# Differential attention: score matmuls over all 128 rows in place of half-height pairs

## The chip, the cores and the metric

The kernel runs on one core of a Trainium2 chip. The metric is the device time of one execution in microseconds (us), as the median over several runs. A core has TensorE (PE: matmuls, with a separate row PEld for the loads of the stationary operand), VectorE (DVE), ScalarE (ACT), GpSimd (POOL) and SyncE (SP), each with a queue of its own that it works off in order, and 16 DMA engines that these queues can start.

## The reference

A trunk of two layers, each with a half-step SwiGLU feed-forward net, a token mixer and a second half-step net, with adaptive modulation and layer norms around them; 512 positions, width 1024, float32. The mixer of the first layer is a bidirectional state-space scan; that of the second is differential attention, which is where the change lies. Cut to this part:

```
qkv = u @ w_qkv                              # u: 512 x 1024
q, k: (512, 8 heads, 2 maps, 64);  v: (512, 8 heads, 128)
s = einsum('bqhmd,bkhmd->bhmqk', q, k) / 8   # per head two maps, contraction over 64
s = s - slope[h] * |pos_q - pos_k|
p = softmax(s)
w = p[map 0] - lam * p[map 1]
o = rms_norm(w @ v, subln_g) * (1 - lambda_init);  out = o @ w_out
```

## The kernel before

All activations lie transposed, features on the 128 partitions and 512 positions along the columns. To keep float32 accuracy with float32r operands, every operand is split in two parts: hi, a rounded copy that ACT writes, and lo = x - hi, which DVE writes. A product is then three matmuls, hi x hi, hi x lo and lo x hi (`mm3`, line 160 of the profile, for all projections). `split_act` and `split_into` make the two parts from a PSUM tile (lines 147 and 148 without a scale, 151 and 152 with one).

Tiles are allocated from pools by a tag. `big` gives 128 x 512 tiles from a pool of 32; PSUM has 8 banks: four "acc" for projections, two "mid", two "ln". The order of the instructions on each engine is not the order of the source: a planner of the framework sets it when the program is built, from priorities in source order, a model of the durations and the free slots of the pools. On the chip each queue is then fixed and works with semaphores.

Attention (`attention`) loops over 8 heads. For each head, `unit_qk(h, 0)` projects q (24 matmuls of 128 x 512, for the two maps at once: map 0 on partitions 0 to 63, map 1 on 64 to 127) and scales it by 1/8, `unit_qk(h, 1)` projects k. The units of head h + 1 are interleaved with the four steps of head h. One step (`score_step`) takes 128 queries: it makes the scores of both maps against all 512 keys, in one "mid" bank for each map. There are six matmuls: for each pair of parts (hi, hi), (hi, lo) and (lo, hi) one for each map, with 64 rows of the stationary and of the moving operand each, rows 0 to 63 for map 0 and rows 64 to 127 for map 1 (line 933). DVE adds the distance term and takes the row maximum (line 936, one for each map), ACT the exponential (943), DVE normalizes and subtracts the maps (944 to 947). `turn_step` transposes the result on PE (955) and splits it (147, 148); `values` multiplies with V on PE (160), takes squares on ACT and sums them on PE (972), POOL takes the power of -1/2 (241), PE broadcasts it (247), DVE scales (978, tile "o"), and a split follows. Weights come through SP's queue (line 93) and are split by lines 117 and 118; POOL starts no DMA in this kernel.

Of the kernel before, what the change touches and what calls it, by code (L numbers as in the profile page):

```python
# [9 lines left out]
F32 = mybir.dt.float32  # L10
F32R = mybir.dt.float32r
AF = mybir.ActivationFunctionType
ALU = mybir.AluOpType
# [33 lines left out]
def hybrid_trunk(tc, xT, cb, par, cst, adaw, wgu, wdn0, wdn1, wdn2, wdt, win, wso, wqk, wv, wao, dist_in, dtp, lam_in, out):  # L47
    nc = tc.nc
# [13 lines left out]
    def big(dt=F32, name="big"):  # L62
        return ap.tile([P, T], dt, tag="a", name=name)

    def tmp(name="tmp"):
        return tp.tile([P, T], F32, tag="t", name=name)

    def acc(tag="acc"):
        return ps.tile([P, T], F32, tag=tag, name=tag, bufs=BANKS[tag])
# [21 lines left out]
    def load(src, n=1024):  # L91
        raw = wp.tile([P, 1024], F32, tag="raw", name="raw", bufs=4)
        nc.sync.dma_start(raw[:, :n], src)
        return raw[:, :n]
# [6 lines left out]
    def split(raw, where=None):  # L101

        n = raw.shape[-1]
        if where == "a":
            hi, lo = [], []
            for o in range(0, n, T):
                r = raw[:, o : o + T]
                h, l = big(F32R, "wah"), big(F32R, "wal")
                x = nc.scalar.activation(h, r, AF.Copy)
                y = nc.vector.tensor_tensor(out=l, in0=r, in1=h.bitcast(F32), op=ALU.subtract)  # L110
                for a, b in zip((x, y), behind):
                    tc.add_manual_dep(a.ins, b.ins.name, NOSYNC, reason="inputs before weights")
                hi.append(h)
                lo.append(l)
            return [(hi[c // T][:, c % T : c % T + P], lo[c // T][:, c % T : c % T + P]) for c in range(0, n, P)]
        hi, lo = ring()
        nc.scalar.activation(hi[:, :n], raw, AF.Copy)  # L117
        nc.vector.tensor_tensor(out=lo[:, :n], in0=raw, in1=hi[:, :n].bitcast(F32), op=ALU.subtract)  # L118
        return Unit(hi, lo, n)
# [20 lines left out]
    def split_act(src, scale=None):  # L140
        hi, lo = big(F32R, "hi"), big(F32R, "lo")
        split_into(hi, lo, src, scale)
        return hi, lo

    def split_into(hi, lo, src, scale=None):
        if scale is None:
            x = nc.scalar.activation(hi, src, AF.Copy)
            y = nc.vector.tensor_tensor(out=lo, in0=src, in1=hi.bitcast(F32), op=ALU.subtract)  # L148
            return x, y
        else:  # L150
            nc.scalar.activation(hi, src, AF.Copy, scale=scale)
            nc.vector.scalar_tensor_tensor(
                out=lo, in0=src, scalar=scale, in1=hi.bitcast(F32), op0=ALU.mult, op1=ALU.subtract
            )
# [11 lines left out]
    def proj(o, w, u, m=P, cols=FULL, prev=None):  # L166
        for a, b in cols:
            prev = mm3(
                o[:m, a:b], [(w[k][0], w[k][1], u[k][0][:, a:b], u[k][1][:, a:b]) for k in range(len(u))], prev
            )  # L170
        return prev
# [706 lines left out]
    def attention(n):  # L878
# [8 lines left out]
        for j in range(2):  # L887
            nc.vector.scalar_tensor_tensor(
                out=lt[:, 256:320], in0=lt[:, 128 * j : 128 * j + 64], scalar=1.0, in1=lt[:, 128 * j + 64 : 128 * j + 128],
# [8 lines left out]
        qks, V = {}, {}  # L898

        def unit_qk(h, e, cols=FULL, pre=None):  # L900
            def f():
                pp = acc()
                proj(pp, pre or split(load(wqk[h, e])), u, cols=cols)
                qks[h, e] = split_act(pp, 0.125 if e == 0 else None)
            return f

        def unit_v(p_):
# [14 lines left out]
            return f  # L922

        def score_step(h, i, bt):
            (qh, ql), (kh, kl) = qks[h, 0], qks[h, 1]
            sm = sp.tile([P, 8], F32, tag="sm", name="sm", bufs=4)
            ss, pt = [acc("mid") for _ in range(2)], []
            c = slice(i * P, (i + 1) * P)

            for j, (a, b) in enumerate(((qh, kh), (qh, kl), (ql, kh))):  # L930
                for m in range(2):
                    r = slice(m * 64, m * 64 + 64)
                    nc.tensor.matmul(ss[m], lhsT=a[r, c], rhs=b[r, :], start=j == 0, stop=j == 2)  # L933
            for m in range(2):
                p = tmp("p")
                nc.vector.tensor_tensor_reduce(
                    out=p, in0=ss[m], in1=bt[:, 384 - i * P : 896 - i * P], scale=1.0, scalar=-3.0e38,
                    op0=ALU.add, op1=ALU.max, accum_out=sm[:, m : m + 1],
                )
                pt.append(p)  # L940
            nc.vector.tensor_scalar(out=sm[:, 2:4], in0=sm[:, 0:2], scalar1=-1.0, scalar2=None, op0=ALU.mult)
            for m in range(2):
                nc.scalar.activation(pt[m], pt[m], AF.Exp, bias=sm[:, 2 + m : 3 + m], accum_out=sm[:, 4 + m : 5 + m])
            nc.vector.reciprocal(sm[:, 6:8], sm[:, 4:6])
            nc.vector.tensor_tensor(out=sm[:, 7:8], in0=sm[:, 7:8], in1=nlam, op=ALU.mult)
            nc.vector.tensor_scalar(out=pt[0], in0=pt[0], scalar1=sm[:, 6:7], scalar2=None, op0=ALU.mult)
            nc.vector.scalar_tensor_tensor(
                out=pt[0], in0=pt[1], scalar=sm[:, 7:8], in1=pt[0], op0=ALU.mult, op1=ALU.add
            )
            return pt[0]  # L950
# [46 lines left out]
        for h in range(8):  # L997
            bt = bp.tile([P, 896], F32, tag="bt", name="bt")
            nc.scalar.activation(bt, dist, AF.Copy, scale=-(2.0 ** -(h + 1)))
            wh = bp.tile([P, 4, T], F32R, tag="wth", name="wth")  # L1000
            wl = bp.tile([P, 4, T], F32R, tag="wtl", name="wtl")
            todo = []
            if h < 7:
                todo += [unit_qk(h + 1, e) for e in range(2)]
            if h in (1, 3, 5):
                todo.append(unit_v((h + 1) // 2))
            if h == 7:
                todo.append(outp)
            for i in range(4):
                w = score_step(h, i, bt)  # L1010
                back.append(lambda i=i, w=w, wh=wh, wl=wl: turn_step(i, w, wh, wl))
                if i == 3:
                    back.append(lambda h=h, wh=wh, wl=wl: values(h, wh, wl))
                    back.append(lambda: rests.pop(0)())
                if todo:
                    todo.pop(0)()
                while len(back) > 2 and not (h == 7 and i == 3):
                    back.pop(0)()
# [10 lines left out]
    for d in range(KT):  # L1029
# [9 lines left out]
        for o in (hl[0], uf):  # L1039
            x = nc.scalar.activation(o, res[d], AF.Identity, bias=shift[0][:, d : d + 1], scale=onep[0][:, d : d + 1])  # L1040
# [122 lines left out]
```

## Time and profile before

| | |
|---|---|
| median of 3 runs | 2211.13 us (2209.78 to 2213.06) |
| the profiled execution, its own time | 2214.77 us |
| its span, first to last instruction | 2213.0 us |
| granted TensorE clock, mean | 0.993 |
| PE, PEld busy | 2156.0 us (97%), 1858.7 us (84%) |
| DVE, ACT, POOL busy | 1701.8 us (77%), 1059.4 us (48%), 136.2 us (6%) |
| DMA queues | 88384 packets, 294.81 MB on the one hardware queue; no software queue |

Busy times are shares of the whole span. Attention takes from about 1570 to 1830 us of it. Matmuls are pipelined: the recorded duration of one overlaps with the next, so what a matmul takes of PE's time is read from start to start.

### The profile page before, as it was taken

To read this page: it belongs to the slowest core of one execution; us is meant where nothing else is said; L and a number is where in the kernel's file an instruction comes from. 1 tells how busy PE (TensorE), PEld (TensorE's weight loads), DVE (VectorE), ACT (ScalarE), POOL (GpSimd) and SP (SyncE) were. 2 spreads that over 40 slices of the span, in tenths; PEclk is the share of its full clock that TensorE was granted. 3 is DMA by queue.
4 is the path that set the end of the run, shared out by engine and by line. 5 is a ranking of instruction groups with operands and counts; after the bars stand their busy time and mean duration, and the time that the engine had idled before them with its cause. 6 is when DMAs were issued, how large, how long until landed. Compare 5 with 4: busy or idle time off the path is not lost.

```text
span 2213.0 us, 33554 instructions
## 1 busy us (share of the span) xinstructions
PE 2156.0 (97%) x13030; PEld 1858.7 (84%) x13030; DVE 1701.8 (77%) x2948; ACT 1059.4 (48%) x1766; POOL 136.2 (6%) x226
## 2 busy tenths in 40 slices
PE   7999999999999989999999999999999999999998
PEld 5788888966777779989899989899877779989897
DVE  6865568656666689989889988997766689859697
ACT  4422234767656537434355524343845557425253
POOL 0000000034332300000000000000000000000000
PEclk9999999999999999999999999999999999999999
DMA  8865552375445413545543273733211121323231
GB/s 309 284 210 172 189 193 80 100 188 146 143 134 152 120 57 124 195 148 184 169 129 114 84 256 100 245 101 117 69 58 58 58 67 59 124 67 116 86 123 40
DMA packets 88543, 296.95 MB, mean 134 GB/s; under 512 B 9536, under 2 KB 12992, under 8 KB 88384
## 3 DMA queue, kind: packets, MB, share of 16 engines
q1 hardware_dynamic: 88384, 294.81, 41.6%
q8 instruction: 102, 1.67, 0.3%
q14 instruction: 57, 0.47, 0.1%
HBM read 289.53 MB, written 5.24 MB: 133 GB/s over the span
## 4 chain that ended last, share of the span: by engine, by line
PE 78%; DVE 10%; ACT 4%; DMA 3%; issue 3%; POOL 1%; POOLq 0%; ACTq 0%; SPq 0%; DVEq 0%
PE acc L160 64%; PE mid L160 6%; PE mid L783 2%; DMA raw<-in_adaw 1%; DVE raw L178 1%; PE mid L933 1%; DMA raw<-in_wdn 1%; DVE wl L118 1%; DVE raw L459 1%; PE ln L160 1%; DVE wl L450 1%; PE ln L247 1%; POOL E L772 1%; DVE lo L148 1%; PE ln L731 1%
## 5 line engine op out<-in xcount | busy, mean ns | idle before, releaser
L160 PE MATMUL acc<-hi,wh 128*128 128x512 f32 (+1 forms) x1488 | 504.0, 339 | 7.8 <-DVE resid L366 5.3
L160 PE MATMUL acc<-hi,wl 128*128 128x512 f32 (+1 forms) x1488 | 502.7, 338 | 0.0
L160 PE MATMUL acc<-lo,wh 128*128 128x512 f32 (+1 forms) x1488 | 502.1, 338 | 0.0
L160 PE MATMUL acc<-uh,wh 128*128 128x512 f32 (+1 forms) x1256 | 441.4, 352 | 0.1
L160 PE MATMUL acc<-ul,wh 128*128 128x512 f32 (+1 forms) x1256 | 438.9, 350 | 0.8 <-DVE ul L1041 0.8
L160 PE MATMUL acc<-uh,wl 128*128 128x512 f32 (+1 forms) x1256 | 437.5, 349 | 0.8 <-DVE wl L118 0.8
L117 ACT ACTIVATE wh<-raw 128x1024 fp32r<-128x1024 f32 (+1 forms) x234 | 238.8, 1026 | 399.8 <-PE acc L160 212.0
L118 DVE TENSOR_TENSOR wl<-raw,wh 128x1024 fp32r<-128x1024 f32 (+1 forms) x234 | 277.9, 1188 | 83.4 <-ACT wh L117 74.1
L160 PEld LDWEIGHTS acc<-hi,wh 128*128 128x128 f32 x1488 | 281.4, 189 | 44.2 <-issue 5.5
L160 PEld LDWEIGHTS acc<-lo,wh 128*128 128x128 f32 x1488 | 281.4, 189 | 31.1 <-DVE lo L148 1.2
L160 PEld LDWEIGHTS acc<-hi,wl 128*128 128x128 f32 x1488 | 281.5, 189 | 30.7 <-issue 1.2
L449 ACT ACTIVATE wh<-raw 128x1024 fp32r<-128x1024 f32 x162 | 170.7, 1059 | 213.8 <-DVE raw L459 100.0
L160 PEld LDWEIGHTS acc<-uh,wh 128*128 128x128 f32 x1256 | 237.1, 189 | 40.0 <-issue 8.9
L160 PEld LDWEIGHTS acc<-uh,wl 128*128 128x128 f32 x1256 | 237.3, 189 | 34.6 <-issue 3.9
L160 PEld LDWEIGHTS acc<-ul,wh 128*128 128x128 f32 x1256 | 237.4, 189 | 34.3 <-issue 4.4
L450 DVE TENSOR_TENSOR wl<-raw,wh 128x1024 fp32r<-128x1024 f32 x162 | 196.9, 1219 | 29.8 <-ACT wh L449 28.7
L178 DVE SCALAR_TENSOR_TENSOR raw<-raw,cond 128x1024 f32<-128x1024 f32 x144 | 174.7, 1221 | 55.7 <-DMA raw<-in_adaw 54.9
L366 DVE SCALAR_TENSOR_TENSOR resid<-acc,gv,resid 128x512 f32<-128x512 f32 (+1 forms) x172 | 112.4, 659 | 72.7 <-PE acc L160 72.5
L459 DVE TENSOR_TENSOR raw<-raw 128x512 f32<-128x512 f32 x216 | 148.0, 688 | 4.5
L312 POOL TENSOR_TENSOR rr<-vr,mhalf 128x2 f32<-128x2 f32 x12 | 8.8, 732 | 1545.2 <-DVE vr L308 1545.2
L160 PE MATMUL mid<-uh,wh 128*128 128x256 f32 (+2 forms) x332 | 94.9, 286 | 1.9 <-DVE up L491 1.9
L160 PE MATMUL mid<-uh,wl 128*128 128x256 f32 (+2 forms) x332 | 93.9, 283 | 0.0
(264 smaller groups left out, 3724.5 us busy)
## 6 DMA issues: line engine op xcount, KB each, us to landing
raw<-in_wgu SPq DMA_DIRECT2D x176, 512.0 KB, 4.2
raw<-in_adaw SPq DMA_DIRECT2D x144, 512.0 KB, 4.5
raw<-in_wdn SPq DMA_DIRECT2D x64, 448.0 KB, 3.6
raw<-in_win SPq DMA_DIRECT2D x40, 512.0 KB, 3.6
raw<-in_wdn SPq DMA_DIRECT2D x32, 512.0 KB, 4.5
rw<-scr SPq DMA_DIRECT2D x32, 512.0 KB, 5.4
ch<-scr SPq DMA_DIRECT2D x32, 256.0 KB, 3.5
raw<-in_wso SPq DMA_DIRECT2D x16, 512.0 KB, 3.5
```

Of the source, the lines that this page charges most:

```text
L117: nc.scalar.activation(hi[:, :n], raw, AF.Copy)
L118: nc.vector.tensor_tensor(out=lo[:, :n], in0=raw, in1=hi[:, :n].bitcast(F32), op=ALU.subtract)
L148: y = nc.vector.tensor_tensor(out=lo, in0=src, in1=hi.bitcast(F32), op=ALU.subtract)
L160: last = nc.tensor.matmul(o, lhsT=a, rhs=b, start=start and j == 0, stop=j == n - 1, skip_group_check=not start)
L178: nc.vector.scalar_tensor_tensor(out=raw, in0=raw, scalar=1.0, in1=cond, op0=ALU.mult, op1=ALU.mult, accum_out=mods[l][:, j : j + 1],)
L247: nc.tensor.matmul(o[:, j * P : (j + 1) * P], lhsT=cols[:, j : j + 1].broadcast_to([P, P]), rhs=ident, start=True, stop=True)
L366: nc.vector.scalar_tensor_tensor(out=res[d][:, a:b], in0=pd[:, a:b], scalar=gvec[n][:, d : d + 1], in1=res[d][:, a:b], op0=ALU.mult, op1=A ...
L449: nc.scalar.activation(x[0], r, AF.Copy)
L450: nc.vector.tensor_tensor(out=x[1], in0=r, in1=x[0].bitcast(F32), op=ALU.subtract)
L459: nc.vector.tensor_tensor(out=o, in0=x, in1=y, op=ALU.add)
L731: nc.tensor.matmul(pst, lhsT=bt[:, i * P : (i + 1) * P], rhs=xd, start=o == 0, stop=o == 1)
L783: nc.tensor.matmul(py[hh * 64 : (hh + 1) * 64, cc], lhsT=lhs, rhs=rhs, start=k == 0, stop=k == 2)
```

## The change

For each map of a head, k becomes one tile of 128 partitions: the hi part on the map's own 64 partitions and the lo part on the other 64. q becomes two tiles for each map: hi, and lo, each present on both halves of the partitions; ACT and DVE write the map's own half, and a DMA that POOL starts copies it to the other half. A contraction over 128 rows with the hi tile of q then gives hi x hi + hi x lo, and one with the lo tile lo x hi + lo x lo. So a step has four matmuls of full height, two for each map, the first map's ahead of the second's; the term lo x lo, which the kernel before leaves out, comes with it. The space for the descriptors of software DMAs goes from 1024 to 2048.

```diff
@@ unit_qk, def f @@
                 pp = acc()
                 proj(pp, pre or split(load(wqk[h, e])), u, cols=cols)
-                qks[h, e] = split_act(pp, 0.125 if e == 0 else None)
+                qks[h, e] = []
+                for m in range(2):
+                    r, o = (slice(j * 64, j * 64 + 64) for j in (m, 1 - m))
+                    if e == 1:
+                        k = big(F32R, "kk")
+                        nc.scalar.activation(k[r], pp[r], AF.Copy)
+                        nc.vector.tensor_tensor(out=k[o], in0=pp[r], in1=k[r].bitcast(F32), op=ALU.subtract)
+                        qks[h, e].append(k)
+                    else:
+                        hi, lo = big(F32R, "qh"), big(F32R, "ql")
+                        split_into(hi[r], lo[r], pp[r], 0.125)
+                        for x in (hi, lo):
+                            nc.gpsimd.dma_start(x[o].bitcast(F32), x[r].bitcast(F32))
+                        qks[h, e].append((hi, lo))
             return f
@@ score_step @@
-            (qh, ql), (kh, kl) = qks[h, 0], qks[h, 1]
             sm = sp.tile([P, 8], F32, tag="sm", name="sm", bufs=4)
             ss, pt = [acc("mid") for _ in range(2)], []
             c = slice(i * P, (i + 1) * P)
-
-            for j, (a, b) in enumerate(((qh, kh), (qh, kl), (ql, kh))):
-                for m in range(2):
-                    r = slice(m * 64, m * 64 + 64)
-                    nc.tensor.matmul(ss[m], lhsT=a[r, c], rhs=b[r, :], start=j == 0, stop=j == 2)
+            for m in range(2):
+                for j, q in enumerate(qks[h, 0][m]):
+                    nc.tensor.matmul(ss[m], lhsT=q[:, c], rhs=qks[h, 1][m], start=j == 0, stop=j == 1)
@@ kernel @@
-    nc = bacc.Bacc("TRN2", target_bir_lowering=False, num_devices=1, dynamic_dma_scratch_size=1024)
+    nc = bacc.Bacc("TRN2", target_bir_lowering=False, num_devices=1, dynamic_dma_scratch_size=2048)
```

## Rows read from the trace of the kernel before

**Rows 1.** Page, part 1: busy us, share of the span, instructions.

```profile
PE 2156.0 (97%) x13030; PEld 1858.7 (84%) x13030; DVE 1701.8 (77%) x2948; ACT 1059.4 (48%) x1766; POOL 136.2 (6%) x226
```

**Rows 2.** Windows, two heads: length, PE, PEld, DVE, ACT, POOL busy, clock, DMA.

```profile
1673.00:1731.00 58.00, 57.61 (x329) 45.30 (x328) 40.08 (x98) 30.74 (x61) 2.01 (x2) 1.00 0.17 55
```

**Rows 3.** Timeline of PE, a projection's second matmul: start, duration, instruction.

```profile
1579.51 0.39 PE L160 MATMUL acc<-ul,wh 128*128 128x512 f32 x1
```

**Rows 4.** Timeline of PE, from the projection's last matmul over one score step.

```profile
1584.53 0.39 PE L160 MATMUL acc<-uh,wl 128*128 128x512 f32 x1
1584.84 0.50 PE L933 MATMUL mid<-hi 64*128 64x512 f32 x2
1585.18 0.40 PE L933 MATMUL mid<-lo,hi 64*128 64x512 f32 x2
1585.41 0.40 PE L933 MATMUL mid<-hi,lo 64*128 64x512 f32 x2
1585.74 0.50 PE L160 MATMUL acc<-uh,wh 128*128 128x512 f32 x1
1586.08 0.40 PE L160 MATMUL acc<-ul,wh 128*128 128x512 f32 x1
```

**Rows 5.** Timeline of PE, a step whose second map starts later.

```profile
1653.40 0.50 PE L933 MATMUL mid<-hi 64*128 64x512 f32 x1
...
1653.80 0.49 PE L933 MATMUL mid<-hi 64*128 64x512 f32 x1
...
1654.69 0.50 PE L160 MATMUL acc<-uh,wl 128*128 128x512 f32 x1
```

**Rows 6.** Timeline of PE, a step in three pieces.

```profile
1637.77 0.50 PE L933 MATMUL mid<-hi 64*128 64x512 f32 x1
1638.20 0.49 PE L160 MATMUL ln<-wth,hi 128*128 128x512 f32 x1
1638.62 0.49 PE L933 MATMUL mid<-hi 64*128 64x512 f32 x1
...
1639.05 0.50 PE L160 MATMUL ln<-wtl,hi 128*128 128x512 f32 x1
...
1641.82 0.73 PE L933 MATMUL mid<-hi,lo 64*128 64x512 f32 x2
1642.48 0.50 PE L160 MATMUL acc<-uh,wh 128*128 128x512 f32 x1
```

**Rows 7.** Groups by line and shape, 1560 to 1833: count, busy us, mean ns.

```profile
L148 DVE TENSOR_TENSOR lo<-acc,hi 128x512 fp32r<-128x512 f32 x16 | 11.0, 685 | 0.1
L147 ACT ACTIVATE hi<-acc 128x512 fp32r<-128x512 f32 x16 | 9.4, 588 | 3.8 <-PE acc L160 3.8
```

**Rows 8.** Timeline of all engines, about a k split: in brackets the idle time before.

```profile
1651.19 0.68 DVE L148 TENSOR_TENSOR lo<-acc,hi 128x512 fp32r<-128x512 f32 x1
...
1651.79 0.74 DVE L978 SCALAR_TENSOR_TENSOR o<-o,l,ln 128x512 f32<-128x512 f32 x1
...
1652.44 0.68 DVE L936 CUSTOM_DVE_ANT_0 p<-mid,bt 128x512 f32<-128x512 f32 x1
...
1652.58 0.42 PEld L955 LDWEIGHTS ln<-csts,p 128*128 128x128 f32 x4 [0.56 <-DVE o L978]
...
1653.05 0.68 DVE L936 CUSTOM_DVE_ANT_0 p<-mid,bt 128x512 f32<-128x512 f32 x1
```

**Rows 9.** Timeline of POOL and PE, one head's power and its broadcast.

```profile
1644.11 1.01 POOL L241 TENSOR_TENSOR rr<-rv,mhalf 128x4 f32<-128x4 f32 x1 [32.64 <-DVE rv L239]
...
1648.98 1.05 PE L247 MATMUL ln<-csts,rr 128*128 128x128 f32 x8
```

**Rows 10.** DMA issues by line: count, KB each, median us from issue to landing.

```profile
lam<-in_lam SPq DMA_DIRECT2D x1, 128.0 KB, 3.8
```

**Rows 11.** Timeline of DVE and PE, head 0: q's subtraction and the first step.

```profile
1570.86 0.69 DVE L152 SCALAR_TENSOR_TENSOR lo<-acc,hi 128x512 fp32r<-128x512 f32 x1 [1.47 <-ACT hi L151]
...
1578.28 0.50 PE L933 MATMUL mid<-hi 64*128 64x512 f32 x2
```

## The prediction

> **What bounds the kernel now.** The page's first part comes first: TensorE (PE) is busy for 97% of the span, VectorE (DVE) for 77% [rows 1]. A busy PE says little by itself, since matmuls overlap, so the stage that is changed was read next, by windows. [...] The third view is PE's timeline, read from start to start, since a recorded duration contains the overlap with the next matmul.
>
> **The price of a full-height matmul.** From the second of a projection's 24 matmuls (start 1579.51, [rows 3]) to the last (1584.53, first of [rows 4]) are 22 intervals in 5.02 us: 0.228 us each for 128 rows and 512 columns.
>
> **What the six half-height matmuls cost.** The two maps use rows 0 to 63 and 64 to 127, and the rows come in pairs ("x2"): a pair starts within one slot, 0.34, 0.23 and 0.33 us after one another [rows 4]. The six therefore do not take six slots, and "four in place of six" is not a saving of a third. They take three slots, of which the first and last are stretched, and the neighbours pay too: the full-height matmul ahead has 0.31 us to the next start instead of 0.228 (+0.08), and the one behind 0.34 (+0.11). With 0.90 us for the step itself, an unbroken step costs 0.08 + 0.90 + 0.11 = 1.09 us. [...]
>
> Of the 32 steps (8 heads, 4 blocks of queries), 17 have this form. In 8, the second map starts 0.40 us behind the first, as its PSUM bank is still being read, and the pairs come apart [rows 5]: 1653.40 to 1654.69 is 1.29, with the neighbours 1.29 + 0.08 + 0.11 = 1.48. In 3, the planner has laid full-height matmuls between pieces of a step [rows 6]: 0.43 + 0.43 + 0.66 for the pieces, 0.42 - 0.228 = 0.19 for the lone full-height one in between, two more entries at 0.08 and two exits at 0.11, together 2.09. The last 4 are in two pieces; I price them as the 8. Sum: 17 x 1.09 + 12 x 1.48 + 3 x 2.09 = 18.5 + 17.8 + 6.3 = 42.6 us.
>
> **What takes their place.** 32 steps of four matmuls of the shape that the projections around them have: 128 x 0.228 = 29.2 us, wherever the planner puts them, since there is no other height to change to. PE's queue gets shorter by 42.6 - 29.2 = 13.4 us. This is a choice: the trace shows no full-height matmul in this place, and I take the projection's. The bounds are 0.228 and the 0.34 that each first one after a change takes; the second would make it 43.5, no gain at all.
>
> Not all of it arrives. In the 8 steps of [rows 5] the wait for the bank stays: DVE's two reads of the scores start 0.61 us apart (1652.44 and 1653.05, [rows 8]), the first map's two matmuls cover 0.46 of that, so 0.15 us x 8 = 1.2 us remain (0 if DVE is earlier, as the first map's scores are now ready two slots sooner).
>
> **The splits of q and k.** Each of the 16 units had one ACT copy (0.588 us) and one DVE subtraction (0.685, [rows 7]); both are now made twice on 64 partitions with the same 512 columns. I take the full duration for half the partitions, since every row of the trace has its time from the columns; below that, half. DVE gets 16 operations more, at its spacing of 0.60 us (1651.19 to 1651.79, [rows 8]) 9.6 us; ACT 16 x 0.588 = 9.4 us. Over a 58 us stretch DVE goes from 40.1 to 42.5 (four units), ACT from 30.7 to 33.1, so neither becomes the bound on average. What counts is where PE waits behind one: in [rows 8] the k subtraction runs at 1651.19, the head's output scaling (o, L978) behind it at 1651.79, and PE's transposes sat idle 0.56 us until it freed their bank. A second subtraction in front makes this 0.60 longer. This stands once in each of three such stretches, and one like it in head 1: 4 x 0.60 = 2.4 us. Ends: 0 (the planner places them elsewhere) and all 16 pairs exposed, 9.6 + 9.4 = 19.0. I take 2.4, as PE has its own work queued at the other places.
>
> **The transfers.** Per head POOL issues four DMAs, 64 partitions x 2 KB each, that copy q's parts to the other half. The trace has no DMA from POOL. Nearest rows: POOL's only work here takes 1.01 us [rows 9], and a transfer of the same 128 KB lands 3.8 us after its issue [rows 10]. Four in a row are then 4 x 1.01 + 3.8 = 7.8 us. For heads 1 to 7, q is projected beside the first step of the head before; the key projection (24 x 0.228 = 5.5 us) and three more steps lie between, so nothing waits. In POOL's queue stands also the power for the output norm; four issues ahead of it cost at most 4 us, and its broadcast comes at 1648.98 on PE, 3.9 us after the power ended at 1645.12 [rows 9]: covered but for a tenth. Head 0 has no such lead: its subtraction starts at 1570.86 and the first step at 1578.28 [rows 11]. With the second subtraction, 1570.86 + 0.69 + 0.60 + 7.8 = 1580.0 for the last part, which is read by the last of the four matmuls, at 1578.28 + 3 x 0.228 = 1579.0: 1.0 us late, behind which wait the next head's projection and all of PE. Ends: 0 and 5 us (issues twice as dear). [...] The larger descriptor scratch is space only.
>
> **Sum.** -13.4 + 1.2 + 2.4 + 1.0 = -8.8 us. The profiled execution took 2214.8 us (span 2213.0), so its successor would take 2206.0; that execution is 3.6 above the median of the runs, 2211.1, and against the median the time is 2202.3 us. Clock and everything ahead of attention stay.
>
> **Rivals.**
> *Given back (about the same).* The gain is there on PE, but the planner's new order and the longer splits eat it: with 8 to 12 of the 19.0 us exposed instead of 2.4, the sum is -3 to +1, 2208 to 2212 us. For it: DVE's queue is strictly in order and PE already waits on it in [rows 8]. Against it: DVE has 18 us of room in 58.
> *Four slots for three (slower).* Pairs in different row groups run at once, so three slots become four: 32 x 0.228 = 7.3 us more, if the stretched intervals are not due to the height and stay with the score step (their banks, their operands). With the 2.4 and 1.0 that is +10.7, 2221.8 us. It decides from a step of four at 1.19 us with its neighbours: (42.6 - 4.6) / 32, with the losses of the sum. For it: the pairs are plain in [rows 4]. Against it: all long intervals there stand at a change of height, the middle one is 0.23. [...]
> *The splits become the bound (slower).* All 16 pairs exposed (19.0) and head 0 at 5: -13.4 + 1.2 + 19.0 + 5 = +11.8, 2222.9. Against it: [rows 2].
> *More than forecast.* Nothing waits: -13.4, 2197.7.
>
> **How the numbers follow.** Two kernels can be told apart here from about 0.2%, 4.4 us. The forecast (a gain of 5 to 13 us) has 0.68, nothing waits at all 0.04; given back 0.16; four slots 0.06; the splits as the bound 0.06. So faster 0.72, same 0.16, slower 0.12. The range reaches from the whole gain with a little more, 2196, to the end of "given back", 2213, and leaves out the slower cases and a little below.
>
> **What would show it.** In the changed profile the score line should have 128 matmuls of 128 rows, 0.23 us from start to start and 0.23 to their neighbours, no "x2" pairs; two-head stretches of about 55.5 us instead of 58; DVE and ACT two operations for each q and k; a software DMA queue with 32 issues; PE waiting for a DMA at the first step at most. The prediction is wrong if the score matmuls keep intervals over 0.3 us, if PE's idle in attention grows by more than 8 us behind DVE or ACT, or if the time moves outside attention because the planner ordered another stage differently.

## The result and the profile after

The changed kernel takes 2200.84 us (median of 4 runs, 2198.99 to 2204.32) where the kernel before, run beside it, takes 2212.1: 11.3 us less, a ratio of 0.9939 with the interval 0.9926 to 0.9952. A second measurement of the same kernel, among the experiments, gave 0.9944 (0.9931 to 0.9956). The forecast was -8.8 us.

The two profiled executions lie further apart, 2213.0 and 2197.2 us of span, since the stretch ahead of attention, where nothing was changed, differs from one execution to the next. The norm ahead of attention takes its power on POOL at these times, first in the kernel before, then in the changed one:

```profile
1557.43 0.70 POOL L312 TENSOR_TENSOR rr<-vr,mhalf 128x2 f32<-128x2 f32 x1 [11.97 <-DVE vr L308]
...
1553.30 0.69 POOL L312 TENSOR_TENSOR rr<-vr,mhalf 128x2 f32<-128x2 f32 x1 [11.96 <-DVE vr L308]
```

From there to the end of the span are 655.6 us before and 643.9 after (644.4 in the second trace of the changed kernel), 11.2 to 11.7 us less, in line with the medians.

The page's first part, and from its third the queue that is new:

```profile
PE 2142.2 (97%) x12966; PEld 1862.8 (85%) x12966; DVE 1713.7 (78%) x2964; ACT 1069.3 (49%) x1782; POOL 153.2 (7%) x258
...
q0 software_dynamic: 1536, 4.20, 0.8%
```

Against [rows 1], PE has 64 matmuls less and 13.8 us less of recorded time; DVE and ACT have 16 operations more each, 11.9 and 9.9 us. A stretch of two heads runs from one head's power on POOL to that of the head after next (timeline of POOL):

```profile
1637.40 1.04 POOL L241 TENSOR_TENSOR rr<-rv,mhalf 128x4 f32<-128x4 f32 x1 [2.77 <-DVE rv L239]
...
1692.57 1.04 POOL L241 TENSOR_TENSOR rr<-rv,mhalf 128x4 f32<-128x4 f32 x1 [2.81 <-DVE rv L239]
```

That is 55.17 us where the pattern before repeats every 58 [rows 2]; the forecast said about 55.5. The windows of such a stretch (columns as in [rows 2]):

```profile
1666.00:1721.00 55.00, 54.34 (x313) 46.13 (x312) 43.03 (x103) 32.96 (x65) 6.33 (x10) 1.00 0.26 77
```

DVE went from 40.1 to 43.0 us, ACT from 30.7 to 33.0 (forecast 42.5 and 33.1), POOL from 2.0 to 6.3. PE remains the engine without room, busy 54.3 of 55 us as it was 57.6 of 58 before [rows 2].

One step on PE's timeline, to be held against [rows 4]:

```profile
1580.32 0.39 PE L160 MATMUL acc<-uh,wl 128*128 128x512 f32 x1
1580.54 0.39 PE L945 MATMUL mid<-kk,qh 128*128 128x512 f32 x1
1580.77 0.39 PE L945 MATMUL mid<-kk,ql 128*128 128x512 f32 x1
1581.00 0.39 PE L945 MATMUL mid<-kk,qh 128*128 128x512 f32 x1
1581.22 0.39 PE L945 MATMUL mid<-kk,ql 128*128 128x512 f32 x1
1581.45 0.39 PE L160 MATMUL acc<-uh,wh 128*128 128x512 f32 x1
```

No pairs any more, and every interval is 0.22 to 0.23 us, at the boundaries too: 0.91 us for the step, with nothing at the neighbours. Behind a run of 128-column matmuls (transposes or the broadcast) a piece's first interval reads 0.31 to 0.32, but the one ahead of it 0.03 where that run has 0.11, so nothing is added there either.

Where the gain sits is plainest in what the weight loads (PEld) waited for during attention, 1570 to 1790 us: total us, times, longest. "issue" is idle time without a releaser in the trace. Of the kernel before:

```profile
PEld acc L160 <- issue: 8.3, 23, 0.4
PEld mid L933 <- issue: 5.9, 22, 0.4
PEld ln L955 <- issue: 3.0, 9, 0.4
PEld ln L955 <- DVE o L978: 1.7, 3, 0.6
```

and of the changed one:

```profile
PEld ln L247 <- POOL rr L241: 3.2, 3, 1.1
PEld ln L984 <- ACT sq L980: 1.6, 7, 0.3
PEld mid L945 <- DVE sm L948: 1.4, 3, 0.5
...
PEld mid L945 <- issue: 0.6, 3, 0.2
```

Some 17 us of "issue" at the score matmuls and at what stood next to them have shrunk to 0.6. The trace shows no other engine's finish at the end of that time; that it was the change of height itself is what the mixed run below shows. New at the top is a wait for POOL's power (0.7 us in this stretch before).

### The profile page after: what moved, and what is told of

Same layout as the page of the kernel before. It is cut to its first block, busy times and chain, and to the rows that moved or that the text cites. A ratio compares the mean times of both kernels' runs of the same rounds, so it can differ in the third digit from the quotient of the medians.

```text
span 2197.2 us, 33556 instructions
## 1 busy us (share of the span) xinstructions
PE 2142.2 (97%) x12966; PEld 1862.8 (85%) x12966; DVE 1713.7 (78%) x2964; ACT 1069.3 (49%) x1782; POOL 153.2 (7%) x258
## 4 chain that ended last, share of the span: by engine, by line
PE 50%; DVE 8%; issue 3%; ACT 3%; DMA 2%; POOL 1%; ACTq 0%; POOLq 0%; DVEq 0%; SPq 0%
PE acc L160 40%; PE mid L160 6%; DMA raw<-in_wdn 1%; DVE raw L459 1%; PE mid L945 1%; DVE wl L118 1%; DVE wl L450 1%; PE ln L160 1%; DMA raw<-in_adaw 1%; DVE raw L178 1%; PE ln L247 1%; DVE lo L148 1%; DVE resid L316 0%; ACT wh L117 0%; DVE resid L366 0%
## 5 line engine op out<-in xcount | busy, mean ns | idle before, releaser
L160 PEld LDWEIGHTS acc<-uh,wl 128*128 128x128 f32 x1256 | 237.0, 189 | 33.1 <-issue 2.4
```

Source lines behind the costliest of these rows:

```text
L160: last = nc.tensor.matmul(o, lhsT=a, rhs=b, start=start and j == 0, stop=j == n - 1, skip_group_check=not start)
```

## The experiments

The theory: each time PE goes from full to half height and back, it loses some 0.4 us (1.09 for an unbroken step, less three slots of 0.228), and the kernel before paid that at every piece of a step; pairs in different row groups share a slot (0.23 us for the middle pair of [rows 4]). The rivals: it is the number of matmuls, or their order, or the splits and copies matter. "Before" is always the kernel before, run beside. A piece is a run of score matmuls without another matmul between, counted on PE's timeline: 42 in the kernel before.

**The changed kernel again.** No edit.

> The changed kernel as it is, for comparison with the runs beside it: -10 to -13 us against before.

2200.85 us, ratio 0.9944. The following are held against this too.

**Half the rows again for two of four.**

```diff
-                for j, q in enumerate(qks[h, 0][m]):
-                    nc.tensor.matmul(ss[m], lhsT=q[:, c], rhs=qks[h, 1][m], start=j == 0, stop=j == 1)
+                (qh, ql), k, r = qks[h, 0][m], qks[h, 1][m], slice(m * 64, m * 64 + 64)
+                nc.tensor.matmul(ss[m], lhsT=qh[:, c], rhs=k, start=True, stop=False)
+                nc.tensor.matmul(ss[m], lhsT=ql[r, c], rhs=k[r, :], start=False, stop=True)
```

> The changed kernel with the second matmul of each map cut to the map's own 64 rows (lo x hi alone, the term lo x lo left out): four matmuls a step as before this cut, two of them half-height, each between full-height ones. Theory (each change of height costs): a lone half-height matmul took 0.43 us in the kernel before and its neighbours 0.08 and 0.11 more, 0.62 instead of 0.228, so 64 x 0.39 = 25 us more than the changed kernel, +14 against before, though it does less arithmetic. Rival (a matmul costs a slot whatever its height; the old order cost): within 2 us of the changed kernel.

2222.87 us, ratio 1.0050 (1.0037 to 1.0063): 22.0 us more than the changed kernel, for less arithmetic in as many matmuls. The rival is out. Nor can the planner's order be the reason, since the 48 pieces of this run have the lengths of the changed kernel's, one by one. A step on PE's timeline, with line 945 at full height and 946 at half:

```profile
1579.24 0.39 PE L945 MATMUL mid<-kk,qh 128*128 128x512 f32 x1
1579.56 0.49 PE L946 MATMUL mid<-kk,ql 64*128 64x512 f32 x1
1579.98 0.50 PE L945 MATMUL mid<-kk,qh 128*128 128x512 f32 x1
1580.41 0.50 PE L946 MATMUL mid<-kk,ql 64*128 64x512 f32 x1
1580.84 0.50 PE L160 MATMUL acc<-uh,wh 128*128 128x512 f32 x1
```

The intervals are 0.32, 0.42, 0.43 and 0.43 us, 1.60 for four matmuls that take 0.91 at one height. What the loads waited for (1570 to 1840 us) says where:

```profile
PEld mid L946 <- issue: 18.4, 63, 0.4
PEld acc L160 <- issue: 8.0, 33, 0.2
```

That is 0.29 us of idle before 63 of the 64 half-height loads, and 0.24 before the projections' full-height ones behind them.

**Six matmuls of full height.**

```diff
-                for j, q in enumerate(qks[h, 0][m]):
-                    nc.tensor.matmul(ss[m], lhsT=q[:, c], rhs=qks[h, 1][m], start=j == 0, stop=j == 1)
+                qa, qb = qks[h, 0][m]
+                for j, q in enumerate((qa, qb, qb)):
+                    nc.tensor.matmul(ss[m], lhsT=q[:, c], rhs=qks[h, 1][m], start=j == 0, stop=j == 2)
```

> The changed kernel with each map's second matmul made twice (the lo part of q counted double), six full-height matmuls a step. If a full-height score matmul costs one projection slot of 0.228 us and attention hangs on PE's queue (theory), 64 more cost 14.6 us: +3 us against before, +14.6 against the changed kernel. If attention no longer hangs on PE (rival: DVE or ACT sets its pace after the change), less than 8 us over the changed kernel.

2215.05 us, ratio 1.0007 (0.9998 to 1.0017): 14.2 us over the changed kernel, 14.2 / 64 = 0.222 us for each added matmul. A slot costs what a projection's does (0.228), and attention still hangs on PE's queue.

**The six half-height ones map after map.**

```diff
-            for j, (a, b) in enumerate(((qh, kh), (qh, kl), (ql, kh))):
-                for m in range(2):
-                    r = slice(m * 64, m * 64 + 64)
+            for m in range(2):
+                r = slice(m * 64, m * 64 + 64)
+                for j, (a, b) in enumerate(((qh, kh), (qh, kl), (ql, kh))):
```

> The kernel before, with its six half-height matmuls in another order: all three of map 0, then all three of map 1. If pairs in different row groups share a slot (theory), only the last of map 0 and the first of map 1 can still overlap: five slots for three, about 0.46 us more in each of the 17 unbroken steps and less in the others, +8 to +13 us against before. If every matmul takes a slot of its own whatever its rows (rival), the order changes nothing: within 4 us of before.

2214.88 us, ratio 1.0009 (1.0000 to 1.0019): the theory's +8 to +13 is a miss. But the rival's reason is not there either. PE's instructions are now queued map by map, three of map 0 and then three of map 1, and yet the trace shows this:

```profile
1581.74 0.50 PE L933 MATMUL mid<-hi 64*128 64x512 f32 x2
1582.08 0.40 PE L933 MATMUL mid<-lo,hi 64*128 64x512 f32 x2
1582.31 0.40 PE L933 MATMUL mid<-hi,lo 64*128 64x512 f32 x2
```

The same pairs at the same intervals as in [rows 4]: map 1's first matmul runs beside map 0's first, though two others stand between them in the queue; the first pair's record is 0.50 us long, and the next pair starts 0.34 us after it. So sharing a slot is confirmed in a stronger form than I had it; the step's order within a whole piece did not matter in this run.

**Two pairs for three.** The term lo x hi is left out.

```diff
-            for j, (a, b) in enumerate(((qh, kh), (qh, kl), (ql, kh))):
+            for j, (a, b) in enumerate(((qh, kh), (qh, kl))):
...
-                    nc.tensor.matmul(ss[m], lhsT=a[r, c], rhs=b[r, :], start=j == 0, stop=j == 2)
+                    nc.tensor.matmul(ss[m], lhsT=a[r, c], rhs=b[r, :], start=j == 0, stop=j == 1)
```

> The kernel before without the term lo x hi: four half-height matmuls a step, in two pairs. Theory (height changes cost, pairs share a slot): one slot of 0.23 us less a step, 32 x 0.23 = -7.4 us against before, still 2 to 5 us slower than the changed kernel, though it has half as many slots: an unbroken step takes 0.67 us and 0.19 at its neighbours, 0.86, against 0.91. Rival (height costs nothing, what helped is that a step has four matmuls instead of six): as fast as the changed kernel, -11 us or more.

2213.66 us, ratio 1.0000 (0.9992 to 1.0009). Neither: a third of the score matmuls gone, and no gain. The rival (the number of matmuls) is out, since these are four, as in the changed kernel; the theory's -7.4 us did not come. The reason that the trace offers is that the planner, with other durations, laid the steps out in 55 pieces instead of 42. A whole step, and further down one of a single map:

```profile
1575.51 0.50 PE L933 MATMUL mid<-hi 64*128 64x512 f32 x2
1575.85 0.40 PE L933 MATMUL mid<-lo,hi 64*128 64x512 f32 x2
1576.17 0.50 PE L160 MATMUL acc<-uh,wh 128*128 128x512 f32 x1
...
1590.19 0.50 PE L933 MATMUL mid<-hi 64*128 64x512 f32 x1
1590.53 0.39 PE L933 MATMUL mid<-lo,hi 64*128 64x512 f32 x1
1590.85 0.50 PE L160 MATMUL acc<-ul,wh 128*128 128x512 f32 x1
```

Both take 0.66 us: here a piece with one map cost what a piece with two did, each with intervals of 0.34 and 0.32 us for two slots of 0.228, and there are 13 pieces more to go into and out of. The changed kernel has 48 pieces, with 0.22 to 0.23 us at their boundaries as inside a projection.

**Fewer pieces at half height.** A step's first matmul also waits for the read of the second bank (`read[0]` holds the last of DVE's reductions).

```diff
-                    nc.tensor.matmul(ss[m], lhsT=a[r, c], rhs=b[r, :], start=j == 0, stop=j == 2)
+                    x = nc.tensor.matmul(ss[m], lhsT=a[r, c], rhs=b[r, :], start=j == 0, stop=j == 2)
+                    if j == 0 and m == 0 and read[0] is not None:
+                        tc.add_manual_dep(x.ins, read[0].ins.name, SYNC, reason="both banks free")
...
+                read[0] = nc.vector.tensor_tensor_reduce(
```

> The kernel before with one wait more: a step's first half-height matmul waits until both banks have been read, so that the second map does not start late and fewer steps come apart: 26 whole steps for 17 whole and 8 apart. Theory: 26 x 1.09 + 6 x 1.5 = 37.3 us instead of 42.6, -5 us against before; -2 if PE then waits for DVE at some of them. That would be the part of the gain that comes from whole steps, the rest from the height itself. Rival (the wait for the bank only moves): within 1.5 us of before.

2210.67 us beside 2214.3, ratio 0.9985 (0.9975 to 0.9994): 3.6 us less by the medians, between the theory's two figures; by the interval 1.3 to 5.5 us less, which leaves the rival (within 1.5 us) hardly any room. The pieces went from 42 to 38, and the time from a piece's start to the next foreign one, summed, from 36.0 to 31.9 us. So some part of what the change gained, a third by the medians, is to be had by fewer pieces alone; that the rest needs the height is the mixed run's showing, not this one's.

**A block for each step.**

```diff
-            for j, (a, b) in enumerate(((qh, kh), (qh, kl), (ql, kh))):
+            with tc.tile_critical():
+                for j, (a, b) in enumerate(((qh, kh), (qh, kl), (ql, kh))):
...
```

> The kernel before with the six half-height matmuls of every step bound into one block, so that the planner lays nothing between them: 32 unbroken steps for 17. Theory: 32 x 1.09 = 34.9 us for 42.6, -5 to -8 us against before, if the wait for the second bank does not eat it; 3 us or more short of the changed kernel. [...]

2247.45 us, ratio 1.0156 (1.0142 to 1.0169): an inconclusive run. All 32 steps are whole, but the block waits at its head, once for each step and 1.0 us on average, which drowns what was to be seen:

```profile
PEld mid L934 <- issue: 32.8, 32, 3.4
```

**Splits by halves, and the copies,** with the half-height matmuls of the kernel before. The first run has the loop of splits alone, the second the DMAs too, into tiles that nothing reads (and, as in the changed kernel, the larger space for their descriptors).

```diff
-                qks[h, e] = split_act(pp, 0.125 if e == 0 else None)
+                hi, lo = big(F32R, "hi"), big(F32R, "lo")
+                for m in range(2):
+                    r = slice(m * 64, m * 64 + 64)
+                    split_into(hi[r], lo[r], pp[r], 0.125 if e == 0 else None)
+                qks[h, e] = hi, lo
+                if e == 0:                      # second run only
+                    for x in (hi, lo):
+                        d = big(F32R, "dup")
+                        for m in range(2):
+                            r, o = (slice(j * 64, j * 64 + 64) for j in (m, 1 - m))
+                            nc.gpsimd.dma_start(d[o].bitcast(F32), x[r].bitcast(F32))
```

> The kernel before with its half-height matmuls, but q and k split map by map on 64 partitions: 16 more operations on ACT and on DVE, nothing else. Theory: 0 to +2.4 us against before (the term of the sum). Rival (the splits are exposed in DVE's queue): +5 to +19 us.

> As the run with split halves, with the 32 DMAs of q from POOL too, into tiles that nothing reads. Theory: within 1.5 us of the run without them, as nothing waits for a copy and POOL has room. Rival (the transfers, or POOL's work for them, disturb DVE or the norm's power): 3 us or more above it.

2216.45 us, ratio 1.0018 (1.0010 to 1.0027), and 2215.89, ratio 1.0019 (1.0009 to 1.0030). The splits bring +3.2 us by the medians, just above the term's 0 to 2.4 and below the rival's 5 to 19, whose edge the interval (2.2 to 6.0 us) still touches; the copies bring nothing. Of the 3.2, the steps themselves account for 2.3: the planner laid them in 45 pieces, and their time went from 36.0 to 38.4 us. That leaves about 1 us for the splits; what they cost with full-height steps was not measured by itself.

**Without the copies:** ACT and DVE write both halves.

```diff
                         split_into(hi[r], lo[r], pp[r], 0.125)
-                        for x in (hi, lo):
-                            nc.gpsimd.dma_start(x[o].bitcast(F32), x[r].bitcast(F32))
+                        nc.scalar.activation(hi[o], pp[r], AF.Copy, scale=0.125)
+                        nc.vector.scalar_tensor_tensor(
+                            out=lo[o], in0=pp[r], scalar=0.125, in1=hi[r].bitcast(F32), op0=ALU.mult, op1=ALU.subtract
+                        )
```

> The changed kernel without DMAs: ACT and DVE write q's parts on both halves of the partitions, straight from PSUM, 16 more operations on each; PE's matmuls are the same. Theory (both the copies and the splits lie beside PE's work): within 2 us of the changed kernel, -9 to -13 against before. Rival 1 (the DMA path costs): faster than the changed kernel by 2 us or more. Rival 2 (DVE is near its limit after the change): slower by 3 us or more.

2204.46 us, ratio 0.9959 (0.9947 to 0.9972): 3.6 us slower than the changed kernel by the medians, which is rival 2 and a miss of the theory's 2 us; but the two intervals overlap, and from the power of the norm ahead of attention to the end its trace has 2.3 to 2.8 us more, so it is not settled between them. Rival 1 is out. With 16 operations more, the loads wait for DVE again, for o and for k:

```profile
PEld ln L969 <- DVE o L992: 1.7, 3, 0.6
...
PEld mid L947 <- DVE kk L912: 0.9, 2, 0.6
```

The DMAs look the better way here, by 2 to 4 us: they keep this work out of DVE's queue.

**More matmuls between the squares and the broadcast,** in all heads, then only in those that project V.

```diff
-                while len(back) > 2 and not (h == 7 and i == 3):
+                while len(back) > 3 and not (h == 7 and i == 3):          # first run
+                while len(back) > 2 + h % 2 and not (h == 7 and i == 3):  # second run
```

> The changed kernel with one more piece held back before the transposes, the values and the scaling are called, so that the planner has other matmuls to lay between a head's sum of squares and the broadcast that waits for POOL's power. PE waited 4.5 us for that power in the changed kernel, 1.5 in the kernel before. Theory (these waits are what is missing from the full 13.4 us): 1 to 4 us faster than the changed kernel. Rival (another wait takes their place): no faster.

> The changed kernel with one more piece held back in the heads that project V, none in the others: 85 to 96 matmuls of 256 columns or 11 of 512 columns lie between each sum of squares and the broadcast that waits for POOL, where the changed kernel has three of 512 columns in every other head. Theory (PE's waits for POOL are a loss of the changed kernel): 1 to 3 us faster than it, and the fastest here. Rival: another wait takes their place, no faster.

2202.69 us, ratio 0.9957 (0.9943 to 0.9970), and 2200.15, ratio 0.9942 (0.9930 to 0.9955), beside the changed kernel's 0.9944: no faster as a whole, twice. In the second, the wait for POOL is gone (1570 to 1790 us):

```profile
PEld ln L984 <- ACT sq L980: 2.4, 6, 0.7
PEld mid L945 <- DVE sm L948: 1.7, 6, 0.3
PEld ln L967 <- DVE o L990: 0.9, 3, 0.3
...
PEld ln L247 <- POOL rr L241: 0.5, 1, 0.5
```

3.2 us have become 0.5, but the waits for the squares, the maxima and o grew by 0.8, 0.3 and 0.9. Yet the traces leave the theory some room: from the norm's power ahead of attention to the end they have 642.7 and 642.0 us, against 643.9 and 644.4 of the changed kernel, 1.2 to 2.4 us less. Ahead of that mark, where nothing was changed, they are longer by more than that (1558.2 and 1559.2 us, against 1553.3 and 1556.2), which would hide it. One trace of each run does not settle so small a difference, and no run beat the changed kernel by more than their interval.

## Why the prediction was right, and where it was off

*Six are not six.* Right: the pairs share a slot (0.34, 0.23 and 0.33 us from pair to pair [rows 4]), and the gain is not a third of the score matmuls. It is what the boundaries cost, as the mixed run shows: with 64 half-height matmuls put back between full-height ones, the kernel is 22 us slower.

*42.6 us before, 29.2 after.* Right in mechanism and size. A slot measured 0.222 us against 0.228; the wait for the second bank, put at 1.2 us, is 1.4 in three places (the DVE sm row above, idle time of the loads). 13.4 - 1.2 = 12.2 us is what the first two terms leave, and the two measurements, 11.3 and 12.4 us by their medians, lie about that.

*Splits on half the partitions take the full duration.* Right, 0.688 us on DVE and 0.587 on ACT for k, beside 0.685 and 0.588 on all 128 [rows 7]; groups by line, 1555 to 1830 us:

```profile
L912 DVE TENSOR_TENSOR kk<-acc,kk 64x512 fp32r<-64x512 f32 x16 | 11.0, 688 | 2.5 <-ACT kk L911 2.1
...
L911 ACT ACTIVATE kk<-acc 64x512 fp32r<-64x512 f32 x16 | 9.4, 587 | 2.6 <-DVE kk L912 2.5
...
L918 POOL DMA_DIRECT2D qh<-qh x16 | 8.8, 547 | 144.6 <-ACT qh L151 142.7 <-DVE p L959 1.9
```

*PE waits 2.4 us more behind DVE.* Mis-sized: the place named, the transposes behind o [rows 8], no longer waits at all. The planner's new order has the transposes elsewhere. What came instead is the loads' wait for POOL, 0.7 us from 1570 to 1790 before and 3.2 in the rows above; when the last experiment took it away, the time as a whole did not fall by more than the runs can tell.

*Head 0 is 1.0 us late for q's copies.* Mis-sized: 0. An issue takes POOL 0.55 us rather than 1.01 (last row above), and the hi copies land 2.5 us after it rather than 3.8 (the view of the tile qh; the lo copies 2.2 by the page's list of DMA issues):

```profile
DMA to landing us min/median/max: 2.1/2.5/3.3
```

The bound from the hardware queue, 3.8 us, was too high. PE ran straight into the first step, and what its loads waited for there, 0.26 us, was k's second subtraction:

```profile
1573.94 0.28 PE L160 MATMUL acc<-wh,ul 128*128 128x256 f32 x1
...
1574.06 0.40 PE L945 MATMUL mid<-kk,qh 128*128 128x512 f32 x1
...
1574.52 0.19 PEld L945 LDWEIGHTS mid<-kk,qh 128*128 128x128 f32 x1 [0.26 <-DVE kk L912]
```

So the two losses of 2.4 and 1.0 us that were in the sum did not come, and -8.8 became -12.2.

*Clock and everything else stay.* Not quite: a loss that the sum did not have, some 1.4 us by the clock at the end of attention (below), takes part of that back, and 11.3 were measured. That the forecast came as near as it did is partly luck: terms that lay on opposite sides of the sum were off. The rivals: "four slots for three" falls with the step's 0.91 us; "the splits become the bound" falls with DVE's 43.0 of 55; "given back" is seen at most in part, in the run that gave DVE 16 operations more.

## What to carry to other kernels

Price a matmul by the interval to the next start, and look at the neighbours: here the half-height matmuls, run in pairs, took three slots of a step where the full-height ones take four, and still cost more, 1.09 us against 0.91, because PE paid some 0.4 us for going into that height and coming out again. Stacking the hi and lo parts of a 64-row contraction makes it one of 128 rows, adds one small term, and here it made the planner's interleaving free (0.22 to 0.23 us at the boundaries). Where an engine other than the bound has to double its splits for it, a DMA from an idle queue can be the cheaper copy, if the data is needed a few us later: here the copies landed 2.2 to 2.5 us after their issue, and the run without them took 3.6 us more by the medians. And where executions differ by a few us ahead of the stage that was changed, compare the traces from a mark behind that part.

## What the runs showed of the hardware that was not expected

PE did not start its matmuls strictly in the order of its queue: with three of map 0 queued ahead of three of map 1, the first ones of both are recorded as one pair of 0.50 us, 0.34 us ahead of the next pair (map-after-map run).

A lone half-height matmul between full-height ones cost 0.42 to 0.43 us to the next start, and a full-height one between two of them 0.43; the loads' idle time before a half-height one was 0.29 us (mixed run).

TensorE's clock fell at the end of attention in the changed kernel, where it had not before. The output projection there waits until DVE's residual sum (line 366) has read an accumulator bank; in the new order PE waited for it once, 3.96 us, where the kernel before has two waits (its row: us, times, longest), and the clock 1.00 from 1809 to 1848:

```profile
PE acc L160 <- DVE resid L366: 2.7, 2, 1.5
```

Timeline of PE in the changed kernel, then windows (the clock is the third column from the end):

```profile
1804.32 0.28 PE L160 MATMUL acc<-lo,wh 128*128 128x256 f32 x1
1804.44 0.28 PE L160 MATMUL acc<-hi,wl 128*128 128x256 f32 x1
1808.67 0.58 PE L160 MATMUL acc<-hi,wh 128*128 128x256 f32 x1 [3.96 <-DVE resid L366]
1809.05 0.41 PE L160 MATMUL acc<-lo,wh 128*128 128x256 f32 x1
1809.26 0.41 PE L160 MATMUL acc<-hi,wl 128*128 128x256 f32 x1
```

```profile
1804.00:1808.00 4.00, 0.71 (x6) 0.51 (x5) 4.00 (x8) 1.45 (x3) 0.00 (x0) 0.83 0.66 247
1808.00:1812.00 4.00, 3.33 (x15) 3.33 (x16) 4.00 (x10) 2.22 (x5) 0.00 (x0) 0.50 0.00 0
```

At the granted clock of 0.50 the matmuls of 256 columns go from 0.12 to 0.21 us apart, 15 in that window, 1.4 us lost, and some more before the clock, 0.82 in the next window, is back at 1.00 in 1816 to 1820. The last two runs above bear on this. In the one with more matmuls in all heads, PE has the two waits again, with the same row as the kernel before, and the clock stays at 1.00 there:

```profile
1808.00:1812.00 4.00, 2.47 (x21) 2.27 (x19) 4.00 (x6) 1.10 (x2) 0.00 (x0) 1.00 0.07 30
```

In the other, the wait is one of 3.1 us, and 1812 to 1816 has the clock 0.50. So the fall goes with the wait in one piece in these runs (3.96 and 3.1 us; with two waits, 1.5 us at the longest, it stayed at 1.00 there). Splitting it did not rid the kernel of it, though: in the first of the two runs the clock fell further on, to 0.50 in 1832 to 1836, and as a whole it was no faster.
